# Beta's transposes leave through the eviction pool's buffers, and the modulation's gate row comes four feature tiles later

## The chip, the cores and the metric

The kernel runs on one core of one Trainium2 chip. A core has TensorE (PE, with its weight loads PEld), VectorE (DVE), ScalarE (ACT), GpSimd (POOL) and SyncE (SP, which here only starts DMA transfers). The metric is the device time of one execution in microseconds, the median of several runs.

## The reference

One layer of a diffusion trunk over 256 context tokens and 2048 latent tokens of width 1024. A single input projection of the modulated norm feeds two mixers: a gated delta rule in chunks, run in both directions, and a windowed attention with rotary positions. Each has a SiLU gate; both are projected, merged by sigmoid gates, projected again and added to x through the modulation's gate. Cut to what the change touches:

```python
shift, scale, gate = jnp.split(jax.nn.silu(c) @ w_mod + b_mod, 3, axis=-1)
h = _rmsnorm(x, norm_w) * (1.0 + scale[:, None]) + shift[:, None]
...
qkv, beta_r, decay_r, kb, vb = _split_cols(h @ w_state, STATE_SIZES)
za, qb, zb, ga, gb = _split_cols(h @ w_rest, REST_SIZES)
...
beta = jax.nn.sigmoid(beta_raw.astype(jnp.float32)).reshape(b, l, 2, GDN_HEADS)
...
kb = kc * bc[..., None]
a_mat = jnp.where(strict, jnp.einsum('nbhik,nbhjk->nbhij', kb, kc) * decay, 0.0)
t_mat = lax.linalg.triangular_solve(a_mat, eye, left_side=True, lower=True, unit_diagonal=True)
...
x = x + gate[:, None] * _merge(ya, yb, ga, gb, w_proj_a, w_proj_b, w_out)
```

So beta scales the rows of a strictly lower triangular matrix in each chunk of 64 tokens, whose inverse (I + A) is needed, and gate is a row of 1024 numbers that only the last addition uses.

## The kernel before

Float32 products are split into a high and a low part, so that a matmul of a tile is three passes of PE (high by high, high by low, low by high). The kernel goes through these stages:

1. To about 441 us: the norm of x, the state's projections, keys and values in feature tiles, with the decays of the chunks beside them.
2. 441 to 640 us, the pass over the queries: `qkv([0..3])` projects four feature tiles (PSUM tile `lps`, L524 to L526, then the short convolution L561 to L565 on ACT and DVE). Beside it `q_pass` makes the attention's queries: `tm_dense` (L362 to L369) projects a block into the PSUM accumulator `tmps`, `qk_norm_rope` norms and rotates it (L393 to L415; L399 is the DVE step that reads `tmps` last), and `q_block` (L469 to L479) splits it into `qh` (cast on ACT L472, rest on DVE L473), transposes it on PE (L476 into `zt`), copies it (ACT L478) and stores it from ACT's queue (L479). `qh` is a tile of the pool `pb` with the tag "st", of which there are two buffers. The keys' copy `st` (stored to `ksp` by L586) and `kTl` go through the same two buffers.
3. Between 1 and 2, `scalars2` (L528 to L544) makes the scans' scalars: L530 on DVE, L535 (PE) and L536 (ACT) for the cumulative decays, and for beta two transposes L541 on PE, copied by ACT with a sign (L543) to a tile `bt` and stored by SP (L544) to `brT` in memory. `scalars2` is called with `pb`, so `bt` has the tag "st" as well.
4. 640 to about 911 us, the gates: `gates(range(24), (2, 3), ...)` runs 24 feature tiles of 128 columns over two groups of 512 tokens (`rest`, `rest_run`; PSUM tile `rps`, L524 to L526). A tile takes about 11.2 us. Its weights come by `weights` (L235 to L247): a load `wr` on SP (L241), a cast `wh` on ACT (L243; L245 on POOL in the scan), and the rest `wl` on DVE (L246). Its result leaves through a tile `rt` of the pool `ev`, tag "rt", two buffers (ACT L816, DVE L818 for the first eight tiles; store L819). `matr` (L672), read by the decays, and `grow` (L228) have the same tag.
5. Beside the gates, `base` (L720 to L762) inverts the triangular matrices of two sets of chunks: loads L733 (of `brT`) and L734, steps L737 and L739 that apply beta, then 62 pairs of DVE steps L747 and L749, with POOL's L754 and a store L759. Also beside the gates, `mod_gate` makes the gate row in two halves.
6. From about 911 us the scan over the chunks (`L1002` and on; L1102 makes `v`, which PE's `sps` L1111 takes), gates of the other groups beside it, then attention, the projections and the output.

`mod_gate` is a generator: `gates` takes one step of it per feature tile. A half is eight loads `wmg` of 256 KB on SP (L220; two buffers), scaled by silu(c) on ACT (L221; the first into `gacc`) and added up on POOL (L223), then a matmul with a column of ones over the partitions (L227, `gsum`), the bias loaded into `grow` (L229), two DVE steps (L230, L231) and a store (L232). Each half takes ten steps, so the row is made in the first 20 tiles.

The order in which the instructions of an engine stand isn't the order of the Python code: a scheduler simulates the program and places each instruction in its engine's queue. A tile's buffer is waited for by whoever gets it next. Each engine works strictly in its queue's order; SP and ACT start their DMA transfers in theirs.

## Time and profile before

| what | value |
|---|---|
| median of three runs | 2004.95 us (2003.56, 2004.95, 2009.0) |
| profiled execution, span | 2004.9 us |
| mean granted clock of PE | 0.984 |
| PE busy | 1921.2 us, 96% of the span |
| DVE, ACT, POOL busy | 75%, 40%, 35% |
| DMA, mean over the span | 166 GB/s |

The profiled execution's span is as long as the median run. The profile gives for each instruction its start and duration in us from the span's start, its line (L476), what it writes and reads, and in brackets how long its engine stood idle ahead of it and which instruction ended that. "x8" is a number of records that stand together. "SPq" and "ACTq" are the queues' own instructions, which start a DMA. Busy times are sums over a stretch; the clock (PEclk) is the share of PE's full clock that was granted there.

### The profile page before, as it was taken

To read this page: it belongs to the slowest core of one execution; us is meant where nothing else is said; L and a number is where in the kernel's file an instruction comes from. 1 tells how busy PE (TensorE), PEld (TensorE's weight loads), DVE (VectorE), ACT (ScalarE), POOL (GpSimd) and SP (SyncE) were. 2 spreads that over 40 slices of the span, in tenths; PEclk is the share of its full clock that TensorE was granted. 3 is DMA by queue.
4 is the path that set the end of the run, shared out by engine and by line. 5 is a ranking of instruction groups with operands and counts; after the bars stand their busy time and mean duration, and the time that the engine had idled before them with its cause. 6 is when DMAs were issued, how large, how long until landed. Compare 5 with 4: busy or idle time off the path is not lost. (4 is left out here: it accounts for less than half of the span.)

```text
span 2004.9 us, 32107 instructions
## 1 busy us (share of the span) xinstructions
PE 1921.2 (96%) x10947; PEld 1611.0 (80%) x10947; DVE 1509.2 (75%) x2871; ACT 807.4 (40%) x1998; POOL 692.6 (35%) x768
## 2 busy tenths in 40 slices
PE   6999999989999999999999999999989999999998
PEld 3888888779998778877888888788768888877786
DVE  6979766667776899999777776535587777747888
ACT  5755545554444322111222233224675655532221
POOL 1652210225543202004222233323456444420675
PEclk8999999999999999999999999999999999999999
DMA  7542326764546733537887777755355555456454
GB/s 252 175 127 94 98 87 154 184 162 157 161 143 166 189 113 113 142 90 216 225 255 221 224 213 217 193 176 165 126 187 173 176 162 165 129 165 211 137 169 136
DMA packets 387704, 333.12 MB, mean 166 GB/s; under 512 B 83993, under 2 KB 307537, under 8 KB 386901
## 3 DMA queue, kind: packets, MB, share of 16 engines
q1 hardware_dynamic: 352244, 288.60, 49.9%
q10 hardware_dynamic: 35296, 42.48, 6.0%
q8 instruction: 87, 1.43, 0.3%
q14 instruction: 77, 0.62, 0.1%
HBM read 220.28 MB, written 109.13 MB: 164 GB/s over the span
## 5 line engine op out<-in xcount | busy, mean ns | idle before, releaser
L524 PE MATMUL rps<-hh,wh 128*128 128x512 f32 x768 | 309.6, 403 | 5.0 <-DVE rt L818 3.8
L526 PE MATMUL rps<-hh,wl 128*128 128x512 f32 x768 | 309.0, 403 | 0.0
L525 PE MATMUL rps<-hl,wh 128*128 128x512 f32 x768 | 307.7, 401 | 0.0
L563 DVE SCALAR_TENSOR_TENSOR cacc<-y,cw,cacc 128x512 f32<-128x512 f32 (+1 forms) x224 | 163.2, 750 | 22.9 <-ACT cacc L561 18.9
L524 PEld LDWEIGHTS rps<-hh,wh 128*128 128x128 f32 x768 | 145.7, 190 | 39.8 <-DVE rt L818 4.3
L525 PEld LDWEIGHTS rps<-hl,wh 128*128 128x128 f32 x768 | 145.8, 190 | 32.7
L526 PEld LDWEIGHTS rps<-hh,wl 128*128 128x128 f32 x768 | 145.7, 190 | 32.8
L524 PE MATMUL lps<-hh,wh 128*128 128x512 f32 (+1 forms) x448 | 171.6, 383 | 0.2 <-ACT y L634 0.2
L525 PE MATMUL lps<-hl,wh 128*128 128x512 f32 (+1 forms) x448 | 171.3, 382 | 0.0
L526 PE MATMUL lps<-hh,wl 128*128 128x512 f32 (+1 forms) x448 | 171.2, 382 | 0.0
L945 DVE TENSOR_TENSOR pl<-pt,ph 128x512 fp32r<-128x512 f32 x156 | 105.4, 685 | 41.9 <-ACT ph L943 41.2
L943 ACT CAST ph<-pt 128x512 fp32r<-128x512 f32 x156 | 90.2, 585 | 109.9 <-PE pt L941 76.8
L917 DVE CUSTOM_DVE_ANT_0 pr<-sc,band,sk 128x640 f32<-128x640 f32 (+1 forms) x128 | 106.6, 862 | 34.4 <-PE sc L913 18.3
L816 ACT ACTIVATE rt<-rps 128x512 f32<-128x512 f32 x96 | 57.3, 596 | 181.6 <-PE rps L526 167.8
L749 DVE TENSOR_TENSOR N<-N,btmp 128x62 f32<-128x62 f32 (+30 forms) x124 | 117.2, 945 | 3.0
L747 DVE TENSOR_TENSOR btmp<-N 128x62 f32<-128x62 f32 (+30 forms) x124 | 116.6, 940 | 3.1
L927 POOL TENSOR_SCALAR pr<-pr,sm 128x640 f32<-128x640 f32 (+1 forms) x128 | 99.7, 799 | 55.5 <-DVE sm L925 39.0
L919 ACT ACTIVATE pr<-pr,sm 128x640 f32<-128x640 f32 (+1 forms) x128 | 104.0, 815 | 20.4 <-DVE sm L917 20.4
L246 DVE TENSOR_TENSOR wl<-wr,wh 128x512 fp32r<-128x512 f32 x120 | 92.7, 786 | 24.7 <-POOL wh L245 21.9
L1231 PE MATMUL pps<-yh,wph 128*128 128x512 f32 x256 | 104.8, 411 | 4.3 <-ACT yh L1211 2.2
L245 POOL TENSOR_SCALAR wh<-wr 128x512 fp32r<-128x512 f32 x72 | 48.6, 690 | 170.3 <-PE lps L525 97.2
L1232 PE MATMUL pps<-yl,wph 128*128 128x512 f32 x256 | 100.9, 396 | 0.0
(374 smaller groups left out, 5044.2 us busy)
## 6 DMA issues: line engine op xcount, KB each, us to landing
wr<-in_w_in_dram SPq DMA_DIRECT2D x120, 256.0 KB
kw<-Ksp SPq DMA_DIRECT2D x28, 384.0 KB
x<-vsp SPq DMA_DIRECT2D x36, 256.0 KB
k<-ksp SPq DMA_DIRECT2D x34, 256.0 KB
kT<-kTsp SPq DMA_DIRECT2D x34, 256.0 KB
wm<-in_w_mod_dram SPq DMA_DIRECT2D x16, 512.0 KB
xt<-in_x_dram SPq DMA_DIRECT2D x16, 512.0 KB
dtl<-Dsp SPq DMA_DIRECT2D x32, 256.0 KB
```

What stands on the lines that cost most here:

```text
L524: T.matmul(ps, lhsT=wh[:, k], rhs=xh[:, k], start=k == 0, stop=False)
L525: T.matmul(ps, lhsT=wh[:, k], rhs=xl[:, k], start=False, stop=False)
L526: T.matmul(ps, lhsT=wl[:, k], rhs=xh[:, k], start=False, stop=k == kt - 1)
L563: V.scalar_tensor_tensor(a, y[:, t:t + n], cw[:, m, t:t + 1], a, op0=ALU.mult, op1=ALU.add)
L747: V.tensor_tensor(tv, A[:, m + 1:, m].unsqueeze(2).to_broadcast([h1 + n, r, m]), A[:, m, 0:m].unsqueeze(1).to_broadcast([h1 + n, r, m]), o ...
L749: V.tensor_tensor(A[:, m + 1:, 0:m], A[:, m + 1:, 0:m], tv, op=ALU.add)
L917: V.tensor_tensor_reduce(s_, ps[:, o:768], band[:, b0:b0 + W + 256], -0.125, sk[:, 1, hd:hd + 1], ALU.add, ALU.min, sm[:, h, 1:2])
L919: S.activation(s_, s_, AF.Exp, scale=-1.0, bias=sm[:, h, 1:2], accum_out=sm[:, h, 2:3])
L927: G.tensor_scalar(p[:, h, :W + 256], p[:, h, :W + 256], sm[:, h, 3:4], 1.0, op0=ALU.mult, op1=ALU.mult)
L945: V.tensor_tensor(pl, pt, f32(ph), op=ALU.subtract)
L1231: T.matmul(ps, lhsT=wh[:, k, ms], rhs=hs[k], start=k == 0, stop=False)
L1232: T.matmul(ps, lhsT=wh[:, k, ms], rhs=ls[k], start=False, stop=False)
```

## The change

Two edits. `bt` is taken from the pool `ev`, tag "rt", in place of `pb`'s "st". And `mod_gate` is wrapped in a new generator `behind`, which spends its first four steps on nothing, so that the row's halves are asked for four feature tiles later: the row ends with the last of the 24 tiles.

```diff
@@ scalars2
             T.transpose(ps, br[:, j * 9:j * 9 + 9].rearrange("p c d -> p (c d)"), ident)
-            bt = pool.tile([72, 128], F32, name="bt", tag="st")
+            bt = ev.tile([72, 128], F32, name="bt", tag="rt", bufs=2)
             S.activation(bt, ps, AF.Copy, scale=-1.0)
@@ after gates()
+    def behind(n, jobs):
+        for _ in range(n):
+            yield
+        yield from jobs
+
     with tc.tile_pool(name="gate", bufs=1, reuse_waits="tile") as gp:
-        gates(list(range(24)), (2, 3), mod_gate(gp, ones), by_act=True)
+        gates(list(range(24)), (2, 3), behind(4, mod_gate(gp, ones)), by_act=True)
```

From L840 on, the lines of the changed kernel have numbers five higher. Every engine has the same instructions as before; their places differ in the pass over the queries and at the gate row.

On PE, at the start of the pass over the queries, before (`qh_4925` and `qh_4977` are the first two blocks, `cacc_5027` a convolution's result, `gps` and `zt` PSUM tiles of `scalars2` and of the transposes):

```order
L541 MATMUL zt_4814<-ident_63,br_1919 72x128
L535 MATMUL gps_4792<-g_78,mats_1917 128x72
L535 MATMUL gps_4795<-g_78,mats_1917 128x72
L535 MATMUL gps_4798<-g_78,mats_1917 128x72
L535 MATMUL gps_4801<-g_78,mats_1917 128x72
L535 MATMUL gps_4804<-g_78,mats_1917 128x72
L476 MATMUL zt_4928<-identr_65,qh_4925 128x128 x4
L476 MATMUL zt_4980<-identr_65,qh_4977 128x128 x4
L595 MATMUL zt_5038<-ident_63,cacc_5027 128x128 x4
L366 MATMUL tmps_5280<-qwh_4866,hh1_150 128x256
```

The same place now, in two pieces; between them stand the rest of `tmps_5280`'s 24 matmuls and two of the L535:

```order
L541 MATMUL zt_4814<-ident_63,br_1919 72x128
L476 MATMUL zt_4928<-identr_65,qh_4925 128x128 x4
L366 MATMUL tmps_5280<-qwh_4866,hh1_150 128x256
L367 MATMUL tmps_5280<-qwh_4866,hl1_151 128x256
L368 MATMUL tmps_5280<-qwl_4867,hh1_150 128x256
```

The second piece starts with the last two matmuls of `tmps_5280`; `lps_5332` is a feature tile's projection:

```order
L367 MATMUL tmps_5280<-qwh_4866,hl1_151 128x256
L368 MATMUL tmps_5280<-qwl_4867,hh1_150 128x256
L476 MATMUL zt_4980<-identr_65,qh_4977 128x128 x4
L595 MATMUL zt_5038<-ident_63,cacc_5027 128x128 x4
L535 MATMUL gps_4798<-g_78,mats_1917 128x72
L535 MATMUL gps_4801<-g_78,mats_1917 128x72
L524 MATMUL lps_5332<-hh3_409,wh_4824 128x512
```

Only the first block's transposes stand ahead of `tmps_5280` now; the second block's and the convolution's come behind it, and the L535 are spread behind them.

On ACT, at the same place, before (`bt` are beta's two tiles, `qh` the casts of the two blocks, `npre`, `suf` and `tot` the decays of `scalars2`):

```order
L561 ACTIVATE cacc_5194<-y_5013,cw_1928 128x512
L536 ACTIVATE npre_1921<-gps_4789 128x18x4
L620 COPY pt_4779<-gps_4774 128x512
L543 ACTIVATE bt_4811<-zt_4809 72x128
L536 ACTIVATE suf_1922<-gps_4792 128x18x4
L536 ACTIVATE tot_1923<-gps_4795 128x18x4
L536 ACTIVATE npre_1921<-gps_4798 128x18x4
L564 ACTIVATE y_5013<-cacc_5194 128x512
L536 ACTIVATE suf_1922<-gps_4801 128x18x4
L536 ACTIVATE tot_1923<-gps_4804 128x18x4
L543 ACTIVATE bt_4816<-zt_4814 72x128
L472 CAST qh_4925<-xn_4915 128x4x64
```

And now:

```order
L613 COPY st_4771<-zt_4746 128x512
L472 CAST qh_4925<-xn_4915 128x4x64
L561 ACTIVATE cacc_5194<-y_5013,cw_1928 128x512
L393 ACTIVATE sq_5138<-tmps_5113 128x256
L536 ACTIVATE npre_1921<-gps_4789 128x18x4
L620 COPY pt_4779<-gps_4774 128x512
L543 ACTIVATE bt_4811<-zt_4809 72x128
L543 ACTIVATE bt_4816<-zt_4814 72x128
L472 CAST qh_4977<-xn_4967 128x4x64
L478 COPY qs_4933<-zt_4928 128x512
```

The first cast into `qh` stands ahead of both `bt` now, the second right behind them, and the decays' L536 have come behind the casts.

On SP, at the second half of the gate row, before (`wr` are the tiles' weights):

```order
L241 DMA wr_8364<-in_w_in_dram 128x4x128
L241 DMA wr_8368<-in_w_in_dram 128x4x128
L229 DMA grow_8301<-in_b_mod_dram 1x512
L220 DMA wmg_8512<-in_w_mod_dram 128x512
L220 DMA wmg_8582<-in_w_mod_dram 128x512
L232 DMA gsp_100<-grow_8301 1x512
L220 DMA wmg_8652<-in_w_mod_dram 128x512
L220 DMA wmg_8722<-in_w_mod_dram 128x512
L241 DMA wr_8434<-in_w_in_dram 128x4x128
L241 DMA wr_8438<-in_w_in_dram 128x4x128
```

And now, eight rows further on:

```order
L241 DMA wr_8628<-in_w_in_dram 128x4x128
L241 DMA wr_8632<-in_w_in_dram 128x4x128
L229 DMA grow_8565<-in_b_mod_dram 1x512
L220 DMA wmg_8776<-in_w_mod_dram 128x512
L220 DMA wmg_8846<-in_w_mod_dram 128x512
L232 DMA gsp_100<-grow_8565 1x512
L220 DMA wmg_8916<-in_w_mod_dram 128x512
L220 DMA wmg_8986<-in_w_mod_dram 128x512
L241 DMA wr_8698<-in_w_in_dram 128x4x128
L241 DMA wr_8702<-in_w_in_dram 128x4x128
```

The row's load, its store and the six last `wmg` loads of the second half have passed eight `wr` loads, those of four tiles. The eight loads of the first half and the first two of the second stand ahead of all this, at the same places of SP's queue in both kernels, here the first of them now (`N` and `nb` are base's tiles):

```order
L819 DMA zasp3_120<-rt_7683 128x512
L220 DMA wmg_7931<-in_w_mod_dram 128x512
L220 DMA wmg_8002<-in_w_mod_dram 128x512
L733 DMA nb_9498<-brT_94 64x1x64
L734 DMA N_9497<-Nsp0_89 64x4096
L733 DMA nb_9498<-brT_94 64x1x64
L734 DMA N_9497<-Nsp1_90 64x4096
L819 DMA zasp2_119<-rt_7712 128x512
```

The same holds for the first half's L221 on ACT and L223 on POOL; POOL's seven L223 of the second half have passed one L754. `gsum1` with its L230 to L232 stands at the last tile of the 24, the store L232 right ahead of the scan's first load on SP.

## Prediction

> **What bounds the kernel.** I read the page's sums first, then the windows by stage, then what TensorE (PE) waits for, then the order of time around its longest waits.

> ```profile
> span 2004.9 us, 32107 instructions
> PE 1921.2 (96%) x10947; PEld 1611.0 (80%) x10947; DVE 1509.2 (75%) x2871; ACT 807.4 (40%) x1998; POOL 692.6 (35%) x768
> ```

> PE is busy for 96% of the span, so a change pays only where PE stands idle or runs at a lower clock. The windows (columns: stretch, its length, then each engine's busy time with its count, the granted PE clock, the DMA share and GB/s) show where that is near the change:

> ```profile
> 440.00:480.00 40.00, 35.81 (x247) 32.80 (x245) 30.04 (x71) 19.83 (x68) 17.38 (x19) 0.91 0.56 168
> 480.00:640.00 160.00, 159.82 (x1095) 145.42 (x1094) 117.58 (x275) 69.86 (x209) 76.59 (x88) 1.00 0.49 149
> 672.00:676.00 4.00, 0.18 (x1) 0.18 (x2) 3.96 (x6) 3.51 (x6) 2.18 (x1) 0.87 0.51 153
> 676.00:680.00 4.00, 4.00 (x10) 3.13 (x11) 3.97 (x6) 1.07 (x2) 1.86 (x4) 0.50 0.48 120
> 684.00:920.00 236.00, 236.00 (x1007) 188.04 (x1006) 226.67 (x256) 52.35 (x90) 30.33 (x25) 1.00 0.41 120
> ```

> The pass over the queries starts at about 441 us. Its first 40 us lose 4.2 us to idling and part of the clock; the 160 us behind them are full at clock 1.00, and so is nearly all of the gates' stage (684 to 920). What is won at 441 to 455 is therefore not given back before 640: there PE itself is the bound. Besides, there is one hole at 672 to 676. The waits of PE (us in total, times, longest), first in the window 430 to 660, then 660 to 1000:

> ```profile
> PE zt L476 <- DVE qh L473: 3.8, 2, 3.6
> ...
> ```

> ```profile
> PE rps L524 <- DVE rt L818: 3.8, 1, 3.8
> ...
> PE sps L1111 <- DVE v L1102: 1.4, 1, 1.4
> ```

> Two waits are long: the transposes of the queries wait 3.6 us for qh, and a gate tile waits 3.8 us at 672. The first lies where the first edit is; PE's order of time there (start, duration):

> ```profile
> 441.88 0.34 PE L535 MATMUL gps<-g,mats 128*128 128x72 f32 x2
> ...
> 443.45 1.49 PE L535 MATMUL gps<-g,mats 128*128 128x72 f32 x8 [0.47 <-ACT pt L620]
> 448.53 1.26 PE L476 MATMUL zt<-identr,qh 128*128 128x128 f32 x8 [3.59 <-DVE qh L473]
> 449.59 1.07 PE L595 MATMUL zt<-ident,cacc 128*128 128x128 f32 x4
> 450.32 0.56 PE L366 MATMUL tmps<-qwh,hh 128*128 128x256 f32 x1
> ...
> 452.81 0.41 PE L368 MATMUL tmps<-qwl,hh 128*128 128x256 f32 x1
> ...
> 453.18 0.28 PE L367 MATMUL tmps<-qwh,hl 128*128 128x256 f32 x1
> 453.30 0.28 PE L368 MATMUL tmps<-qwl,hh 128*128 128x256 f32 x1
> ...
> 455.35 0.40 PE L524 MATMUL lps<-hh,wh 128*128 128x512 f32 x1
> ...
> 455.81 0.46 PE L476 MATMUL zt<-identr,qh 128*128 128x128 f32 x4
> 456.10 0.47 PE L526 MATMUL lps<-hh,wl 128*128 128x512 f32 x1
> ```

> And who holds it up, on ACT, DVE and SP's queue:

> ```profile
> 443.23 0.55 SPq L586 DMA_DIRECT2D ksp<-st  x1
> ```

> ```profile
> 447.62 0.88 ACT L472 CAST qh<-xn 128x256 fp32r<-128x256 f32 x2 [1.56 <-DMA brT<-bt]
> ```

> ```profile
> 448.05 0.90 DVE L473 TENSOR_TENSOR qh<-xn,qh 128x256 fp32r<-128x256 f32 x2 [1.56 <-ACT qh L472]
> 448.87 0.42 DVE L399 TENSOR_TENSOR xn<-tmps,ssn 128x256 f32<-128x256 f32 x1
> ```

> Both casts into qh wait until bt's store has landed, since bt sits in the two buffers that qh is to get. Behind DVE's part of qh stands L399, which empties an accumulator; so tmps at 450.32 could not start sooner either, though its data were there.

> **Part 1, bt in the eviction pool.** Nothing is added or removed; bt's two tiles take the buffers "rt", one of which was last matr's, whose readers end with the decays, before this. Nobody else wants those buffers before the gates, so brT's stores (L544) no longer hold up anything. In the new order ACT casts the first qh ahead of both bt, DVE's L473 and L399 move ahead of L563, and PE has only four transposes ahead of tmps.

> How much can that give? From 441.88 to 455.35 are 13.47 us. Idle in them: 3.59 + 0.47 = 4.06. Run slowly: from 450.32 to 453.02 thirteen matmuls lie 0.213 apart, against 0.12 for 453.18 to 453.30, some 1.2 us lost; eight transposes of qh take 1.06 (448.53 to 449.59), against 0.29 for four (455.81 to 456.10), 0.5 lost; the four of L595 take 0.73 to 450.32, some 0.4 lost. Together 4.06 + 2.1 = 6.2 us, the most that this place can yield.

> What is late next? The second qh (qh_4977) now follows ksp<-st in its buffer. That store is issued at 443.23 and its place in SP's queue is the same. For its landing I have bt's 36 KB: issued at 445.89, the cast released at 447.62, 1.7 us; for 256 KB I estimate 2.5, so 445.8. Then a cast and a subtraction, about 0.45 each, give 446.8 for the second four transposes. PE gets there earlier: the first qh, whose input was there (its cast above waits for the DMA alone), is done by about 442.4, behind L530 on DVE; tmps starts at 442.8 and needs 24 x 0.12 + 0.36 for the two L535 put between, until 446.0. PE waits 0.8 to 0.9 us. Its bounds are 0 (the store lands in 1.7) and about 3 (it takes 4.5 in a busy queue). Farther on the blocks of queries follow one another more closely, and I allow 0.3 us for small waits. 6.2 - 0.9 - 0.3 = 5.0 us, and with the bounds 2.9 to 6.2. The 0.9 should not cost clock: ahead of this place PE waited longer and went on at 0.28 per matmul:

> ```profile
> 438.51 0.38 PE L366 MATMUL tmps<-qwh,hh 128*128 128x256 f32 x1 [1.69 <-ACT y L634]
> 438.73 0.28 PE L367 MATMUL tmps<-qwh,hl 128*128 128x256 f32 x1
> ```

> **Part 2, the gate row four tiles on.** The order shows that only half of it moves. The eight wmg loads of the first half, ACT's L221 and POOL's L223 on them keep their places on SP, ACT and POOL, because nothing holds them back but buffers; they stay beside base's loads at 654 to 672. What moves by four tiles is gsum0, the row's load, L230 to L232, then six of the second half's loads with their L221 and L223, and gsum1. The instructions are the same, and PE's two gsum are paid either way: 0 us on PE, if DVE keeps its cover. DVE is the engine beside them (start, duration; the last column is the wait):

> ```profile
> 742.32 1.19 DVE L747 TENSOR_TENSOR btmp<-N 128x992 f32<-128x992 f32 x1
> ...
> 748.90 2.17 DVE L747 TENSOR_TENSOR btmp<-N 128x990 f32<-128x990 f32 x1
> 750.99 0.67 DVE L230 TENSOR_TENSOR grow<-gsum,grow 1x512 f32<-1x512 f32 x1
> ...
> 752.69 1.51 DVE L231 TENSOR_SCALAR grow<-grow 1x512 f32<-1x512 f32 x1
> ...
> 792.66 0.69 DVE L246 TENSOR_TENSOR wl<-wr,wh 128x512 fp32r<-128x512 f32 x1
> ...
> 911.18 1.08 DVE L246 TENSOR_TENSOR wl<-wr,wh 128x512 fp32r<-128x512 f32 x1 [1.33 <-POOL wh L245]
> ```

> ```profile
> 752.24 4.21 POOL L223 TENSOR_TENSOR gacc<-gacc,wmg 128x512 f32<-128x512 f32 x2 [2.22 <-ACT wmg L221]
> ```

> ```profile
> 786.13 0.62 ACT L243 CAST wh<-wr 128x512 fp32r<-128x512 f32 x1 [4.76 <-PE rps L525]
> ...
> 797.33 0.62 ACT L243 CAST wh<-wr 128x512 fp32r<-128x512 f32 x1 [4.76 <-PE rps L525]
> ```

> Beside an L223 a step of base takes 2.17 instead of 1.19: seven adds cost DVE some 7.0 us, and L230 and L231 about 1.1 more (between 0.68 + 0.41 and 2.2). This 8.1 us leaves 747 to 770 and comes back 4 x 11.2 us later (797.33 - 786.13 is a tile). [...] DVE can keep 5.9 of the 8.1 ahead: L246 of 792.66 can run no sooner than the first cast's end, 786.75. So DVE is 2.2 us later there than before, and it idles more than that (58 - 53.05) in the last tiles before the scan:

> ```profile
> 853.00:911.00 58.00, 58.00 (x248) 45.73 (x247) 53.05 (x53) 10.44 (x19) 3.63 (x4) 1.00 0.31 91
> ```

> The second row's L230 and L231 now stand at about 907, just ahead of the wait of 1.33 at 911.18: 1.1 of it is used up. SP's L232 there holds back the scan's first loads (L1004), which before were issued from 910.71 on; gsum1 at 905 plus two steps of base and the row give about 909. I take 0 for part 2, with bounds of -0.5 (less work of POOL's beside the long steps) and +2 (the scan's v late, where PE waits 1.4 already).

> Sum: 2004.9 - 5.0 + 0 = 1999.9; the median of the runs is 2004.95, the same as the span; I say 2000.0.

> **Rivals.** *A, the hole at 672 changes as well* (its clock or all of it).

> ```profile
> 675.82 0.79 PE L524 MATMUL rps<-hh,wh 128*128 128x512 f32 x1 [3.84 <-DVE rt L818]
> 676.41 0.63 PE L525 MATMUL rps<-hl,wh 128*128 128x512 f32 x1
> ...
> 681.53 0.52 PE L525 MATMUL rps<-hl,wh 128*128 128x512 f32 x1
> ```

> Twelve matmuls lie 0.43 apart instead of the gates' 236/1007 = 0.234: 2.4 us, and 3.84 of waiting. If the clock stays up: 2000.0 - 2.4 = 1997.6; if the loads thinned out and the hole went too: 1993.8. Against it: SP's and ACT's orders are unchanged here, and this is the sense in which part 2 doesn't do what it says. For it: both drops came from waits of 3.59 and 3.84, none from 1.69, so half a microsecond less may decide. [...] Chance 0.2.

> *B, the wait is only handed on.* The second qh waits for ksp's store as the first did for brT's, and PE comes to 3 us and more of waiting, with the clock down again (2.1): 6.2 - 3.5 - 2.1 leaves 0.6, 2004.3. For it: SP issues without pause there and 443.23 can't move. Against: PE has tmps to run meanwhile, which covers 3 us. Chance 0.15.

> *C, slower: the second half's adds make wl late.* Place: the tiles from 790 to 820. First-half wl must be there when the next tile starts, 11.2 us after its cast began. In before it came 6.5 + 0.7 after (786.13 to 792.66), so 4.0 us were free. DVE later than before by over 4.0 decides; I expect 2.2. If each add costs DVE 2.0 us instead of 1.0 (its pairs last up to 4.21 on POOL), it is 15.1 - 5.9 = 9.2 late, PE waits 5.2 and loses 2.4 of clock: 2000.0 + 7.6 = 2007.6. Against it: before carried the same adds with DVE no less full, and PE never waited there. Chance 0.1.

> **How the numbers follow.** The forecast has 0.55. Its own range is 1998.2 to 2003.0 (bounds 2.9 to 6.2 and +1). About 0.3%, 6.0 us, is what a measurement of this kernel can tell from no change: faster means under 1998.9, slower over 2011. Faster: nearly all of A (0.2) and the upper fifth of the forecast, 0.11, together 0.31. Slower: only C at its worst, 0.05. The rest, 0.64, is the same. For eight in ten I take 1995.0 to 2006.0, which leaves out the end of A (the whole hole filled) and most of C.

> **What would show it.** In the changed profile: L476 waits under 1 us at about 447, not 3.6, and for the second qh alone; ACT's L472 no longer ends a wait for brT; the clock of 440 to 480 is 0.97 or more; lps of 455.35 starts at about 449; the hole at 672 stands 5 us earlier, with its 3.8; steps of L747 of over 1.8 us stand about 45 us later; PE has no wait from 684 to 905. I am wrong if L476 waits over 2 us, if PE waits for wl between 785 and 825, or if the 5 us are there at 480 and gone at 640.

## The result and the profile after

The changed kernel takes 1993.58 us (median of 20 runs, 1988.19 to 2002.0), the kernel before 2002.93 us (20 runs, 1995.94 to 2009.0). The ratio is 0.9959, 95% interval 0.9949 to 0.9968: 8.2 us less, 6.4 to 10.2. The forecast was 2000.0 us with a range of 1995.0 to 2006.0, so it had the direction and not the size, and the time lies below the range.

The profiled execution of the changed kernel, its head and its windows (columns as before):

```profile
span 1990.4 us, 32103 instructions
PE 1912.3 (96%) x10947; PEld 1602.2 (80%) x10947; DVE 1507.1 (76%) x2871; ACT 805.9 (40%) x1998; POOL 689.5 (35%) x768
```

```profile
440.00:480.00 40.00, 38.26 (x277) 34.78 (x276) 32.18 (x77) 20.13 (x70) 21.85 (x24) 1.00 0.67 194
480.00:640.00 160.00, 159.69 (x1083) 144.61 (x1082) 115.64 (x268) 70.68 (x207) 72.25 (x84) 1.00 0.49 148
...
666.00:670.00 4.00, 0.61 (x3) 0.27 (x2) 3.97 (x6) 3.57 (x6) 2.25 (x1) 0.93 0.56 167
670.00:674.00 4.00, 4.00 (x12) 3.18 (x13) 3.97 (x6) 0.98 (x2) 1.92 (x4) 0.64 0.54 132
...
684.00:920.00 236.00, 236.00 (x1023) 187.35 (x1022) 226.57 (x257) 51.08 (x88) 28.88 (x25) 1.00 0.42 122
```

From 440 to 480 PE is busy for 38.3 us at clock 1.00 (before 35.8 at 0.91). The hole of 672 to 676 has moved to 666 to 670 and is still there. PE's waits from 430 to 660, then from 660 to 1000:

```profile
PE gps L604 <- DMA kTl<-kTsp: 1.6, 1, 1.6
PE tmps L366 <- ACT y L634: 1.0, 1, 1.0
PE zt L476 <- DVE qh L473: 0.3, 1, 0.3
PE rps L524 <- DVE rt L818: 0.2, 1, 0.2
```

```profile
PE rps L524 <- DVE rt L818: 3.4, 1, 3.4
PE mep L1033 <- DVE moff L1030: 1.6, 1, 1.6
PE sps L1116 <- DVE v L1107: 1.1, 1, 1.1
```

Nothing is left of the transposes' wait of 3.6 at this place; the 0.3 belongs to another block, at 531. A load of kTl is late by 1.6 instead, at 469, which the forecast did not have. PE's order of time at the place of the first edit:

```profile
440.52 0.39 PE L535 MATMUL gps<-g,mats 128*128 128x72 f32 x2
440.75 0.38 PE L541 MATMUL zt<-ident,br 128*72 128x128 f32 x2
440.88 0.54 PE L476 MATMUL zt<-identr,qh 128*128 128x128 f32 x4
441.34 0.39 PE L366 MATMUL tmps<-qwh,hh 128*128 128x256 f32 x1
...
444.95 0.54 PE L476 MATMUL zt<-identr,qh 128*128 128x128 f32 x4
...
446.29 0.50 PE L524 MATMUL lps<-hh,wh 128*128 128x512 f32 x1
...
616.55 0.39 PE L526 MATMUL lps<-hh,wl 128*128 128x512 f32 x1
```

From the first L535 to the first lps behind it are 5.77 us, before 13.47; about 1 us of matmuls (four L604, one L535) now comes later. To the last lps of the pass are 176.03 us. Before they are 180.72, from 441.88 to this row:

```profile
622.60 0.39 PE L526 MATMUL lps<-hh,wl 128*128 128x512 f32 x1
```

So the profile shows 4.7 us won in this stretch, and the two profiles differ by 14.5 us in all. Where the other 10 are from was the question for the experiments.

### The profile page after: what moved, and what is told of

Same layout as the page of the kernel before. It is cut to its first block, busy times and chain, and to the rows that moved or that the text cites. A ratio compares the mean times of both kernels' runs of the same rounds, so it can differ in the third digit from the quotient of the medians.

```text
span 1990.4 us, 32103 instructions
## 1 busy us (share of the span) xinstructions
PE 1912.3 (96%) x10947; PEld 1602.2 (80%) x10947; DVE 1507.1 (76%) x2871; ACT 805.9 (40%) x1998; POOL 689.5 (35%) x768
## 5 line engine op out<-in xcount | busy, mean ns | idle before, releaser
L524 PE MATMUL rps<-hh,wh 128*128 128x512 f32 x768 | 309.2, 403 | 4.7 <-DVE rt L818 3.5
L526 PE MATMUL rps<-hh,wl 128*128 128x512 f32 x768 | 307.0, 400 | 0.0
L525 PE MATMUL rps<-hl,wh 128*128 128x512 f32 x768 | 305.9, 398 | 0.0
L563 DVE SCALAR_TENSOR_TENSOR cacc<-y,cw,cacc 128x512 f32<-128x512 f32 (+1 forms) x224 | 164.1, 753 | 21.4 <-ACT cacc L561 17.8
L524 PEld LDWEIGHTS rps<-hh,wh 128*128 128x128 f32 x768 | 144.7, 188 | 40.1 <-DVE rt L818 5.0
L524 PE MATMUL lps<-hh,wh 128*128 128x512 f32 (+1 forms) x448 | 171.8, 383 | 0.3 <-ACT y L634 0.3
L525 PE MATMUL lps<-hl,wh 128*128 128x512 f32 (+1 forms) x448 | 171.5, 383 | 0.0
L526 PEld LDWEIGHTS rps<-hh,wl 128*128 128x128 f32 x768 | 144.6, 188 | 33.0
L526 PE MATMUL lps<-hh,wl 128*128 128x512 f32 (+1 forms) x448 | 171.0, 382 | 0.0
L525 PEld LDWEIGHTS rps<-hl,wh 128*128 128x128 f32 x768 | 144.9, 189 | 31.9
L747 DVE TENSOR_TENSOR btmp<-N 128x62 f32<-128x62 f32 (+30 forms) x124 | 116.2, 937 | 3.1
L246 DVE TENSOR_TENSOR wl<-wr,wh 128x512 fp32r<-128x512 f32 x120 | 92.8, 786 | 23.8 <-POOL wh L245 21.8
L245 POOL TENSOR_SCALAR wh<-wr 128x512 fp32r<-128x512 f32 x72 | 48.6, 689 | 167.9 <-PE lps L525 97.2
L1238 PE MATMUL pps<-yh,wpl 128*128 128x512 f32 x256 | 101.0, 396 | 0.0
```

Of the source, the lines that this page charges most:

```text
L524: T.matmul(ps, lhsT=wh[:, k], rhs=xh[:, k], start=k == 0, stop=False)
L525: T.matmul(ps, lhsT=wh[:, k], rhs=xl[:, k], start=False, stop=False)
L526: T.matmul(ps, lhsT=wl[:, k], rhs=xh[:, k], start=False, stop=k == kt - 1)
L563: V.scalar_tensor_tensor(a, y[:, t:t + n], cw[:, m, t:t + 1], a, op0=ALU.mult, op1=ALU.add)
L747: V.tensor_tensor(tv, A[:, m + 1:, m].unsqueeze(2).to_broadcast([h1 + n, r, m]), A[:, m, 0:m].unsqueeze(1).to_broadcast([h1 + n, r, m]), o ...
L1238: T.matmul(ps, lhsT=wl[:, k, ms], rhs=hs[k], start=False, stop=k == 3)
```

## The experiments

In all tables "stretch" is from the first L535 to the last lps of the pass over the queries, "scan" from the first sps to attention's first av, "attention" from there to its last av, each from one profile; the interval of the ratio is of 95%. A half-clock window is a stretch of 3.41 us in which the profile has the granted clock at 0.5 (446.27 to 449.68 in the kernel before is one).

**The first edit alone.**

```diff
-            bt = pool.tile([72, 128], F32, name="bt", tag="st")
+            bt = ev.tile([72, 128], F32, name="bt", tag="rt", bufs=2)
```

> Only the first edit: beta's tiles in the eviction pool; the gate row stays where it was. PE's order in the pass over the queries is that of the changed kernel. Theory 1 (the prediction's terms, with the wait for the keys' store struck out, which the changed profile doesn't show): 6 to 7 us less than before, ratio 0.9965 to 0.9970, the first feature tile's lps about 8 us earlier with 1 us of matmuls still to come, and the whole of it kept to the end. Theory 2 (the second edit has a share in the result): 4 to 5 us here, ratio about 0.9978, and the rest with the second edit. Theory 3 (the 14.5 us between the two profiles are mostly chance of single executions): the ratio here is that of the changed kernel, 0.996, within the interval.

Measured: 0.9958 (0.9944 to 0.9973), stretch 175.10, scan 433.4. The effect is here with the first edit alone. Theory 2's 0.9978 lies just outside the interval, which holds Theory 1's 6 to 7 us as well as Theory 3.

**The second edit alone.**

```diff
-        gates(list(range(24)), (2, 3), mod_gate(gp, ones), by_act=True)
+        gates(list(range(24)), (2, 3), behind(4, mod_gate(gp, ones)), by_act=True)
```

> Only the second edit: the gate row's steps four tiles later; beta's tiles stay in the queries' pool. Theory 1: 0 us, ratio 0.999 to 1.001; the hole at 672 stays with about 3.8 us of waiting and half clock behind it. Theory 2: 2 to 4 us less, ratio 0.998 to 0.999, and in the profile PE's waits between 660 and 960 shrink by as much.

Measured: 0.9996 (0.9982 to 1.001), stretch 180.72, scan 438.3. PE's waits from 430 to 1000 in its profile, the long ones:

```profile
PE zt L476 <- DVE qh L473: 3.6, 1, 3.6
...
PE rps L524 <- DVE rt L818: 3.3, 1, 3.3
```

Both holes are there, and the time is the time of before: the second edit does nothing that can be measured, within an interval of 3.6 us less to 2.0 us more.

**The kernel before, twice more** (with the first and the third group of runs).

> The kernel before, unchanged, timed against itself: ratio 1.000. Its profile beside the earlier one shows how much two executions of one kernel differ by stage. Theory 3 expects that some of the 7 us by which the changed kernel's profile is shorter behind 940 us (scan and attention, whose orders did not change) shows here as well: differences of 2 us and more from 940 to 1790. Theories 1 and 2 need no such differences, but then 7 us behind 940 would have to come from the change.

> The kernel before a third time, for a further profile without the edit. Theory A: its scan lies anywhere from 433 to 440, and the stretch from the first L535 to the last lps is 180.7 to 181.1 as in the other three. Theory B: the scan takes 437 or more, with two or three half-clock windows in it.

Measured: 1.001 (0.9993 to 1.0026), stretch 181.07, scan 437.1; and 1.0001 (0.9988 to 1.0013), stretch 181.45, scan 433.9 without any half-clock window in it. So a scan as short as with the edit occurs without it, which Theory B of the last of these runs had excluded, and three profiles of one kernel differ by 6.5 us in the scan, as Theory 3 expected, while the stretch keeps within 0.7 us.

**The gate row's loads really held back.** On the changed kernel:

```diff
-            dma(wr, src[k * 128:(k + 4) * 128].rearrange("(k p) c -> p k c", p=128))
+            last_wr[0] = dma(wr, src[k * 128:(k + 4) * 128].rearrange("(k p) c -> p k c", p=128))
...
-                dma(wm, ins["w_mod"][0, k * 128:(k + 1) * 128, cs_])
+                with tc.issue_after(last_wr[0].ins):
+                    dma(wm, ins["w_mod"][0, k * 128:(k + 1) * 128, cs_])
```

> Both edits, and each load of the gate row (wmg) is also kept on SP behind the last weight load (wr) of the tile that asks for it, so that the first half's loads really come four tiles later instead of beside base's loads at 654 to 672. If those loads make the hole at 672 (the prediction's rival A as a thing to do): the hole's 3.4 to 3.8 us and about 1 to 2.4 us of clock go, 4 to 6 us less than the changed kernel. If base's and the tiles' own loads suffice to make the hole: no difference from the changed kernel, or up to 3 us more where the held loads now meet the second set of base's loads or the scan's first.

Measured: 1.0042 (1.0025 to 1.0059), slower than before. The windows around its hole, and the wait:

```profile
628.00:640.00 12.00, 12.00 (x58) 9.71 (x57) 5.72 (x9) 3.41 (x6) 2.55 (x2) 1.00 1.02 221
640.00:654.00 14.00, 14.00 (x61) 11.26 (x61) 7.08 (x16) 1.84 (x3) 0.00 (x0) 1.00 0.97 217
654.00:658.00 4.00, 0.94 (x5) 0.41 (x4) 3.92 (x6) 0.00 (x0) 0.00 (x0) 1.00 0.88 216
```

```profile
PE rps L527 <- DVE rt L821: 3.1, 1, 3.1
```

No wmg load is among these transfers any more, the DMA engines are as full as ever, and the hole stays: the gate row's loads don't make it. The loss is elsewhere: the scheduler put the scan into another order, and the scan takes 455.3 us.

**The stores of the first gate tiles from ACT's queue.** On the first edit:

```diff
-        (dma if m < 8 else adma)(dst[gi][mm], t)
+        (dma if 2 <= m < 8 else adma)(dst[gi][mm], t)
```

> The first edit, and the stores of the first two gate tiles (zasp) start from ACT's queue instead of SP's. It asks why PE waits at 667 to 672: with the gate row's loads held back the hole stayed (3.1 us), so those loads don't make it. ACT waits 10 to 12 us for a store of zasp that SP issues behind base's loads. If the store is late because it lies behind those loads in SP's queue: the hole goes, 3.5 to 5 us and 2 us of clock less than the first edit alone, ratio about 0.993. If the DMA engines are full whichever queue is used (their share is 1.0 there): the hole stays, ratio 0.996. If ACT now waits in its order for DVE's part of the tile: up to 3 us more.

Measured: 1.0031 (1.0015 to 1.0046); PE still waits 4.2 us in the hole. The store is not late because of SP's queue alone. Again most of the loss is in stages reordered behind: scan 443.1, attention 407.3 against 398.2 to 403.5 in the eight profiles of the kernels before and after and of the edits alone.

**Base's second set of chunks loaded later.** On the first edit, behind tile 8 and behind tile 3 (`hold[8]` is the last weight load asked for at tile 8; the lines that note it are left out here, and the second run has `hold[3]`):

```diff
-                dma(nb[p0:p0 + 8 * k], brT[c:c + k, d * 4:d * 4 + 4].rearrange("c h (b t) -> c (h b) t", b=2))
-                dma(N[p0:p0 + 8 * k], Nsp[d][c:c + k].rearrange("c h b r i -> (c h b) r i"))
+                with tc.issue_after(hold[8].ins) if si else nullcontext():
+                    dma(nb[p0:p0 + 8 * k], brT[c:c + k, d * 4:d * 4 + 4].rearrange("c h (b t) -> c (h b) t", b=2))
+                    dma(N[p0:p0 + 8 * k], Nsp[d][c:c + k].rearrange("c h b r i -> (c h b) r i"))
```

> The first edit, and the loads of base's second set of chunks (nb, N; not needed before its first set is done at about 836) are kept on SP behind the weights of the tenth gate tile instead of standing beside the first set's at 632 to 653. The scheduler also moves the steps that apply beta to them, and some of the scan's order. If these 2 MB in small pieces, and DVE's wait for them, make the hole at 667 to 676: the hole goes, 4 to 6 us less than the first edit alone between 640 and 930. If not: the hole stays. What the scan's other order costs is open: the two kernels whose scan was reordered so far lost 10 us and more there, which would turn it into a loss.

> As before it, with the loads behind the weights of the fifth gate tile (about 45 us later than now instead of 100). The same expectation for the hole; the order behind it is another one, so that the two together tell the hole's share from the scan's.

Measured: 0.9985 (0.9971 to 0.9998) and 1.0044 (1.0029 to 1.0059). The hole stays in both (waits for rt of 4.4 and 5.2 us in total), so these loads alone don't make it either; the scans take 441.3 and 443.3, and attention in the second 410.8. None of four tries removed the hole, and its cause is left open.

**Half of the first edit.** On the kernel before:

```diff
-            bt = pool.tile([72, 128], F32, name="bt", tag="st")
+            bt = (ev.tile([72, 128], F32, name="bt", tag="rt", bufs=2) if j else pool.tile([72, 128], F32, name="bt", tag="st"))
```

> Half of the first edit, on the kernel before: only beta's second tile goes to the eviction pool, the first stays in the queries' pool. In the new order the first cast into qh follows the first beta tile's store in its buffer, the second follows the first qh. Theory 1 (the hole at 448 is qh waiting for beta's store): SP can issue that store only at about 445.9, so PE's transposes still wait 3 us or more with half clock behind it, and at most 1.5 us are gained; ratio 0.999 to 1.000. Theory 2 (the gain comes from the two casts or from the order around them, whichever buffer): 4 us and more.

Measured: 0.9976 (0.9963 to 0.999), stretch 179.26, 1.7 less than before. Theory 1 had the wait too long: it is 1.8, and not for beta's store at all. Theory 2 fits the ratio (4.8 us, 2.0 to 7.4) but not the stretch. ACT's cast into the first qh with the step ahead of it, and SP's stores of the keys and of beta:

```profile
442.70 0.22 ACT L536 ACTIVATE tot<-gps 128x72 f32<-128x72 f32 x1
442.91 0.40 ACT L472 CAST qh<-xn 128x256 fp32r<-128x256 f32 x1
```

```profile
440.37 0.55 SPq L586 DMA_DIRECT2D ksp<-st  x1
...
443.02 0.93 SPq L544 DMA_DIRECT2D brT<-bt  x2
```

The cast runs before beta's store is even issued. In the trace it waits for the semaphore of the keys' store instead, whose last update comes at 442.89, 0.02 us ahead of it. ACT's order holds it nearly as long: the decays' L536 that the scheduler left ahead of it runs until 442.92. This run can't tell the two apart. Of the hole of before, 1.56 us are ACT's wait for beta's store; about 2 are the casts' place in ACT's order (the last step ahead of them ends at 446.05, 1.1 us after PE stopped) and their way through ACT and DVE (0.9). That the scheduler chose this order because of the stores is an inference from the orders, not shown by itself.

**The first edit alone, again, and both edits, again.**

> The first edit alone once more, for a second profile and more executions. The stretch from the decays' first matmul (L535) to the last lps was 5.1 and 5.6 us shorter in the two profiles with the edit than in the three without. Theory A (the further 2 to 3 us of the measured 6.5 to 10 are chance): the ratio comes nearer to 0.9973, and the half-clock windows behind 940 us, 2 and 3 with the edit against 5 or 6 without, are again 4 to 6. Theory B (the later stages really run better): ratio 0.996 again, 2 or 3 windows again.

> The changed kernel once more, for a further profile with the edit. Scan (from its first sps to attention's first av) with the edit so far 436.9, 433.4 and 435.6, without 440.4, 437.1 and 438.3. Theory A (chance of where the clock's windows fall): the further profile lies anywhere from 433 to 440 with 1 to 3 half-clock windows in it. Theory B: below 437 with at most one.

Measured: 0.9969 (0.9953 to 0.9984), stretch 174.39, scan 435.6; and 0.9956 (0.9939 to 0.9973), stretch 174.69, scan 434.5 with one half-clock window in it. Behind 940 us the two profiles have two and three half-clock windows. Neither run decides between its theories: the first ratio lies between the two that were expected, with two windows as in Theory B, and the second scan fits both.

**The first edit and useless matmuls** of 128x512, in `scalars2`:

```diff
         V.tensor_tensor(brs, br, suf, op=ALU.mult)
+        pad = psum("gps", [128, 512], name="pad")
+        for k in range(22):
+            T.matmul(pad, lhsT=identr, rhs=hh[0][:, k % KT], start=k == 0, stop=k == 21)
```

> The first edit, and 22 more matmuls of 128x512 (of use to nobody: their sum isn't read) at the end of beta's and the decays' matmuls in the pass over the queries; behind 640 us the order and the waits are those of the kernel before. They cost PE 22 x 0.233 = 5.1 us and give back what the edit saved there. Theory A: ratio 0.9995 to 1.0005. Theory B, and the gain behind 940 comes with the queries' order and not with the time: 2 to 3 us less than before, 0.9985 to 0.999.

Measured: 0.9989 (0.9974 to 1.0003), stretch 178.91, 3.9 more than the mean of the four with the edit and 2.1 less than without it. The ratio's 2.2 us agree with these 2.1, so nothing further need have come with the queries' order; the interval (5.2 us less to 0.6 more) is too wide to exclude it. That is Theory A's sense, though its number, the full 5.1 given back, missed: the padding also filled the wait for kTl, which is gone from this profile.

**The kernel before and the same useless matmuls.** The edit is the same, on the kernel before.

> The kernel before (beta's tiles in the queries' pool) with the 22 useless matmuls of 128x512. Here they stand on PE right in the hole, between the last L535 and the transposes that wait for qh. If the hole costs its 3.6 us of waiting and 2.1 us of low clock behind it, 5.1 us of matmuls in it cost nothing: 1.5 us of them stick out, and the clock gives back 2.1; the stretch from the first L535 to the last lps takes 180.4 instead of 181.0 and shows no half-clock window, ratio 0.9995 to 1.0005. If the low clock has another cause than PE's idleness: the stretch takes 182.5, ratio 1.0008. Theory B in another form (the later stages run better after any disturbance of this place): 2 us less than the stretch alone gives, ratio 0.9985 to 0.999.

Measured: 0.9994 (0.9977 to 1.001), stretch 180.83. PE's order of time in it, and the window:

```profile
443.46 5.40 PE L541 MATMUL pad<-hh,identr 128*128 128x512 f32 x22 [0.62 <-ACT suf L536]
448.69 0.81 PE L476 MATMUL zt<-identr,qh 128*128 128x128 f32 x8
449.34 0.62 PE L598 MATMUL zt<-ident,cacc 128*128 128x128 f32 x4
...
452.63 0.39 PE L524 MATMUL lps<-hh,wh 128*128 128x512 f32 x1
```

```profile
440.00:480.00 40.00, 38.78 (x267) 34.71 (x266) 30.80 (x70) 21.07 (x70) 19.82 (x22) 1.00 0.60 177
```

Five microseconds of extra matmuls fill the hole and cost nothing: PE idles 0.62 us there and not 3.6, the clock stays at 1.00, and the eight transposes take 0.65 to the next row instead of 1.06. The low clock behind the hole came from the hole. Its price follows too: 5.1 us of work came in, PE idled 3.1 us less in the stretch (1.2 instead of 4.3), and the stretch is the same within 0.2, so about 2.2 us came back with the clock.

**Beta in a third place.** On the kernel before:

```diff
-            bt = pool.tile([72, 128], F32, name="bt", tag="st")
+            bt = pool.tile([72, 128], F32, name="bt", tag="o")
```

> The kernel before with beta's tiles in a third place: the queries' pool, but the buffers of tag o, which the decays' products and the queries' copies (qs) use. The casts into qh are free of beta, beta's copies wait for the products' stores instead. Mechanism as in the first edit (qh no longer behind beta's store): the wait of 3.6 us goes and the stretch from the first L535 to the last lps takes 175 to 177, unless qs now waits for beta. Theory A: the whole time falls by as much, 4 to 6 us, ratio 0.997 to 0.998. Theory B: 2 us more, 0.996.

Measured: 0.9972 (0.9956 to 0.9987), 5.6 us, stretch 175.62, 5.4 less than before. The eviction pool is not what counts; beta out of the two buffers that the casts use is.

The stretch and the scan together, one profile each:

| kernel | ratio to before | stretch | scan |
|---|---|---|---|
| before; again; third | 1; 1.001; 1.0001 | 180.72; 181.07; 181.45 | 440.4; 437.1; 433.9 |
| second edit alone | 0.9996 | 180.72 | 438.3 |
| both edits; again | 0.9959; 0.9956 | 176.03; 174.69 | 436.9; 434.5 |
| first edit alone; again | 0.9958; 0.9969 | 175.10; 174.39 | 433.4; 435.6 |
| beta in tag o | 0.9972 | 175.62 | 437.1 |

With the first edit the stretch is 175.05 in the mean of four, without it 180.99: 5.9 us, and the groups lie 4.7 us apart at the nearest. This is shown. The scan is 435.1 and 437.4 in the mean, and the groups overlap.

## Why the prediction was wrong

**The place and the mechanism were right.** The hole in front of the queries' transposes was what the first edit could win, its ceiling was worked out as 6.2 us, and 5.9 were measured. What was won at 455 was still there at the end of the stretch, at 617. The marks named for it are there: the clock of 440 to 480 is 1.00, L476 waits less than 0.15 us at this place, and no L472 waits for brT; lps stands at 446.29 and not at about 449, but 1.4 us of that is this execution's earlier start of the stretch.

**The step that failed** is "What is late next": 0.9 us for the second qh behind ksp's store. I took the two buffers to go round in turn. They didn't: the second qh got the first qh's buffer. ACT's casts and SP's store in the changed profile:

```profile
438.47 0.45 ACT L472 CAST qh<-xn 128x256 fp32r<-128x256 f32 x1
...
442.29 0.41 ACT L472 CAST qh<-xn 128x256 fp32r<-128x256 f32 x1
```

```profile
441.92 0.55 SPq L586 DMA_DIRECT2D ksp<-st  x1
```

The second cast starts 0.4 us after that store was issued. In the trace the only semaphore that it waits for is one of PE, and the store's last update comes at 446.41, 4.5 us after its issue. (Before, it took 2.5 us from its issue at 443.23, and over the runs 2.5 to 4.5, so the estimate of 2.5 and the bound of 4.5, for which no row was shown ahead of the result, were sound; no tile here waited for it.)

**Two sizes were off as well, and that the sum without the 0.9 gives just 5.9 is luck.** PE in the stretch, before and after (columns: stretch, its length, PE busy with its count, clock, DMA share, GB/s):

```profile
441.88:622.60 180.72, 176.35 (x1207) 0.98 0.49 150
```

```profile
440.52:616.55 176.03, 173.98 (x1207) 1.00 0.51 154
```

In the four profiles without the edit PE idles 4.2 to 4.4 us in the stretch, in the four with it 0.8 to 2.1: 3.0 us less in the mean. For small waits I had allowed 0.3; kTl's load alone takes 0.4 to 1.6, so that the waits which came are about as long as the 0.9 and the 0.3 together, at another place. The clock was worth more than the 2.1 read from the rows: half of the time in which PE is busy at half clock is 2.3 to 3.1 us without the edit, 2.7 in the mean, and nothing with it. The 3.0 and the 2.7 make 5.7 of the 5.9. So the place held more than the 6.2: 4.3 of idling and 2.7 of clock, 7.0 in the mean.

**The base was off by 2.0 us.** The three runs shown had a median of 2004.95; twenty had 2002.93. Of the 6.4 us between 2000.0 and 1993.58, 2.0 are this, 0.9 are the stretch (5.9 for 5.0), 2.3 are open (below), and 1.2 are that the two medians differ by 9.35 where the ratio gives 8.2. The range was worked out from bounds of costs alone (with +1 at its upper end, where part 2 says +2), and held neither this nor the spread of runs (about 13 us from the lowest to the highest of twenty).

**The rest, 2.3 us** between 5.9 and the ratio's 8.2, I could not put anywhere. The five measurements of kernels with the casts freed have ratios of 0.9956 to 0.9972, in the mean 0.9963, 7.4 us; that leaves 1.5. It is in no stage beyond what profiles of one kernel differ by. The stages behind have the same order. Against an effect behind this place speak the padded kernel with the edit (2.2 us in time, 2.1 in the stretch), beta in tag o (5.6 and 5.4) and the short scan of the third profile of before; one speaks for it, half of the edit (4.8 and 1.7). The half-clock windows behind 940 us are 6, 5, 3 and 5 in the four profiles without the edit and 2, 3, 3 and 2 in those with it, which would be worth up to 1.7 us each (half of 3.41); but the padded kernel before has 2 and beta in tag o 4. It stays open; chance would do, and nothing excludes a small real effect. The 10 us that two profiles differed by behind the stretch were mostly chance in any case.

**Part 2 was right at 0**, as far as the interval of the second edit alone tells, and by its working. Half of the row did not move, and DVE's loss moved with the adds. Beside the step of 748.90 in the prediction ran this add, to 750.02 (the POOL row shown there is the next two):

```profile
747.84 2.18 POOL L223 TENSOR_TENSOR gacc<-gacc,wmg 128x512 f32<-128x512 f32 x1 [2.93 <-ACT gacc L221]
```

Two steps of base in the changed profile and the adds beside them; the first step starts just ahead of the first add:

```profile
789.05 0.80 DVE L747 TENSOR_TENSOR btmp<-N 128x612 f32<-128x612 f32 x1
789.88 1.77 DVE L749 TENSOR_TENSOR N<-N,btmp 128x612 f32<-128x612 f32 x1
```

```profile
789.06 3.75 POOL L223 TENSOR_TENSOR gacc<-gacc,wmg 128x512 f32<-128x512 f32 x2 [2.27 <-ACT wmg L221]
```

A step of 0.80 takes 1.77, the same 1.0 us more as the step of 1.19 did, at the new place. That the loss would move with the adds was shown by no row of before and was an assumption of the forecast; these rows show it. PE has no wait from 684 to 905. Not foreseen was that DVE stands idle 1.35 us for the row's own bias load; that was covered too.

**The rivals.** A: the hole at 672 stayed (3.4 us), and the clock behind it came back sooner:

```profile
669.74 0.80 PE L524 MATMUL rps<-hh,wh 128*128 128x512 f32 x1 [3.39 <-DVE rt L818]
670.33 0.63 PE L525 MATMUL rps<-hl,wh 128*128 128x512 f32 x1
...
672.46 0.58 PE L524 MATMUL rps<-hh,wh 128*128 128x512 f32 x1
```

Seven matmuls at half clock instead of thirteen are some 1.2 us saved in this profile, but the first edit alone waited 4.7 us there; it is no property of the change. A's picture of the cause, the gate row's loads, is refuted by the kernel that held them back. B, the wait handed on, is refuted: L476 doesn't wait there. C, wl too late, is refuted: no wait of PE there.

## What to carry to other kernels

Before a wait is priced as "next in line for that buffer", look at what the built instruction really waits for: a pool under a scheduler is not a ring. A hole of PE that is followed by low clock is worth both (here 4.3 us of idling and 2.7 of clock), and PE work put into it can be free (here 5.1 us of matmuls, with the stretch the same within 0.2). A change of 0.4% needs a stage measured in several profiles; the difference of two whole profiles (14.5 us here, for an effect of 8) says little about where the time came from, and a range has to hold the spread of the base as well.

## What the runs showed of the hardware

```profile
442.86:446.27 3.41, 1.59 (x10) 1.00 0.71 156
446.27:449.68 3.41, 1.15 (x9) 0.50 0.62 182
449.68:453.09 3.41, 3.41 (x18) 0.50 0.70 231
453.09:456.51 3.42, 3.42 (x29) 1.00 0.17 57
```

```profile
661.56:664.98 3.42, 2.21 (x10) 1.00 1.10 346
664.98:668.39 3.41, 2.02 (x9) 1.00 0.32 102
```

In the sixteen profiles, from 300 to 1975 us, a full-clock window in which PE was busy for less than 1.5 us was followed by half clock in 59 cases of 59, one with more than 2.2 us never, and between them in 23 of 143. A half-clock window was followed by another if PE was busy in it for 2.71 us or less (15 cases), and by full clock from 2.85 us on (82 cases). In the profiles before and after alone these counts are 7 of 7, none and 4 of 21, and 3 cases up to 2.56 us and 11 from 3.12 on. The wait of 2.6 us lay across two windows and left PE busy for 2.2 and 2.0 us of them; the one of 2.9 lay mostly in one. These are counts of this kernel's runs, with the profile's modelled ends of matmuls.
